# Routed experts: large and small ones by turns, with the banks of PSUM shared out anew

## The chip, the cores and the metric

The kernel runs on one core of one Trainium2 chip. Its measure is the device time of one execution in microseconds; the median of three runs before the change is 2690.89 us (2690.01 to 2691.46).

## What is computed

A stack of layers over 256 tokens of width 1024 (state space mixer, cross attention, gated MLPs, attention, recurrent hybrids), then a mixture of experts, then a last norm. The change touches only the experts:

```
logits = x @ w_router                     # 256 x 8
top_v, top_i = top_k(logits, 2)           # two experts a token
comb = sum(one_hot(top_i) * softmax(top_v))
y = sum over 8 experts of comb[:, e] * (silu(x @ wg[e]) * (x @ wu[e])) @ wd[e]
```

`wg` and `wu` are 1024 x 3584, `wd` is 3584 x 1024, all f32. The kernel computes products to f32 accuracy with the chip's rounded type fp32r: each f32 operand is split in a high part and a rest, and three of the four products are summed.

## The kernel before

**Experts and slots.** Each expert computes only its own tokens, gathered into slots. The experts are sorted by their count of tokens (except that the first to run is expert 0 in any case), and run in the order `RANKS` of that list. `CAPS` says how many slots each has in the order of running: 128, 128, 64, 128, 128, 64, 128, 64. More tokens than slots would start a second round under an `If` (it isn't entered for these inputs). With 128 slots, high part and rest of the gathered tokens are two operands (`gx`, two tiles). With 64 they stand side by side in one operand of 128 columns, so that one matmul does two products; its two halves are added later by a matmul with a doubled identity (`twice`, in `turn_small`). So an expert of 128 slots needs three matmuls for each block of weights, one of 64 slots two, while the weights to be loaded and converted are the same.

**Steps.** An expert runs in `NG` = 7 steps of 512 of its 3584 hidden columns. `up(x, g, mid)` loads two tiles of 1 MB of the gate weights and two of the up weights and accumulates `eg` and `eu` in a bank of PSUM each; `mid` is called between the two. `step_down` does the down projection of the step before that (`late`): two more tiles of 1 MB, accumulated over all seven steps in two banks `eacc`. Between them the product `ea` (or, with 64 slots, the copies `es`) is transposed by `turn` or `turn_small` into a bank `ept` and split. Every tile of 1 MB is one DMA from SP's queue into a raw buffer and is converted in two halves: ACT casts `whi` (L475), DVE subtracts `wlo` (L476), and the raw buffer is free again. There are `W_BUFS` = 4 converted halves of each kind, so the two engines are at most four halves ahead of PE. `raw_tile` deals raw buffers out by turns: 4 in `ring`, 6 in `raw2`, 3 in `raw3` during the experts.

**Start and end of an expert.** `places(es)` gathers tokens for the one or two experts of a group: it builds selections `pm`, multiplies them with the normed tokens into four banks `mpg`, which ACT and DVE read into `gx`. It is called after step 3 of the expert ahead. `places_back`, at step 4, transposes the selection for the way back into a bank `mpt`. After the last down projection, `back` scales `eacc` into `eyh` and `eyl`, scatters them with eight matmuls through four banks `esc`, and DVE adds these to the residual.

**Order.** The loop in `moe_round` runs over the eight experts one after the other, and over seven steps inside; `GROUPS` says only which experts are gathered together. The framework's planner sets each engine's order from the program's order (earlier instructions have priority), its own costs and the buffers that are free at that point, and it may start a later matmul while an earlier one lacks an operand. On the chip each engine's queue then runs in that fixed order.

**Banks.** PSUM's eight banks are two sets of four: `ps` holds `eacc`, `ept`, `mpg`, `mpt2` and `esc`; `wv` holds `eg` and `eu`.

Of the kernel before, what the change touches and what calls it, by code (L numbers as in the profile page):

```python
# [19 lines left out]
P = 128  # L20
# [8 lines left out]
NE = 8  # L29
# [2 lines left out]
RANKS = [0, 1, 5, 2, 3, 6, 4, 7]  # L32
SMALL = 64
CAPS = [P if r < 5 else SMALL for r in RANKS]
GROUPS = [[0], [1, 2], [3, 4], [5, 6], [7]]

STAGES = ["ssm", "xa0", "ffn0", "cf", "xa1", "ffn1", "ab", "cd", "hy0", "sw", "hy1", "moe", "final"]

# [193 lines left out]

RAW_BUFS = 4
W_BUFS = 4
N_T1 = (13, 6, 4)
N_T2 = (14, 4, 12)
N_SM = 20
LD = 2
FIN = 0
LEAD = 2  # L240
MORE_RAW = (6, 3)
CF_PE = [11, 12, 12, 12, 15, 15, 18, 19]
MP = 3

# [2 lines left out]
def hybrid_stack_kernel(ctx: ExitStack, tc: tile.TileContext, A, out, voff, coff, stages=STAGES):  # L247
# [66 lines left out]
    def g4(name, shape, dt=F32):  # L314
        if "attn" in pools:
            return pools["attn"].tile(list(shape), dt, tag="g4", name=name, bufs=6)
        return pools["work"].tile(list(shape), dt, tag="g4", name=name, bufs=5)

    def sm(name, shape, dt=F32):
        return pools["work"].tile(list(shape), dt, tag="sm", name=name, bufs=N_SM)  # L320
# [1 line left out]
    def ps(name, shape=(P, 2, T)):  # L322
        return psum.tile(list(shape), F32, tag="ps", name=name, bufs=4)
# [7 lines left out]
    def f32v(ap):  # L331
        return ap.bitcast(F32)
# [1584 lines left out]
    def x_by_tokens():  # L1917
        px = [ps("xtp", (P, 512)) for _ in range(4)]
        for t in range(2):
            for k in range(KD):  # L1920
                pe.transpose(px[2 * t + k // 4][:, (k % 4) * P : (k % 4 + 1) * P], xT[:, k, t * P : (t + 1) * P], ident)
        for i in range(4):
            act.copy(xtok(i // 2, i % 2), px[i])
# [4 lines left out]
    def moe_round(rnd, hth, htl, sel0, sel, comb, rest=None):  # L1928
# [30 lines left out]
        def places(es):  # L1959

            w = len(es) * P
            pm = [t1("pm", (P, T), F32R) for _ in range(2)]
            for t in range(2):
                for u, e in enumerate(es):
                    c = CAPS[e]
                    dve.tensor_scalar(
                        pm[t][:, u * P : u * P + P].rearrange("p (a b) -> p a b", b=c),
                        bc2(iota[:, :c], P // c), (sel if e else sel0)[:, t, e : e + 1], 0.0, op0=OP.is_equal, op1=OP.add,
                    )

            pgs = []
            for k2 in range(4):
                pg = ps("mpg")
                for j in range(2):
                    k = 2 * k2 + j
                    cs = slice((k % 4) * P, (k % 4 + 1) * P)
                    for t in range(2):
                        r = pm[t][:, :w]
                        mm(pg[:, j, :w], hth[2 * t + k // 4][:, cs], r, j == 0 and t == 0, False)
                        mm(pg[:, j, :w], htl[2 * t + k // 4][:, cs], r, False, j == 1 and t == 1)  # L1980
                pgs.append(pg)
            r = []
            for u, e in enumerate(es):
                c = CAPS[e]
                gx = [g4("gx", (P, KD, P), F32R) for _ in range(2 if c == P else 1)]
                for k2 in range(4):
                    ks = slice(2 * k2, 2 * k2 + 2)
                    o = u * P
                    hi = gx[0][:, ks, :c]
                    lo = gx[1][:, ks, :] if c == P else gx[0][:, ks, c:]  # L1990
                    act.copy(hi, pgs[k2][:, :, o : o + c])
                    dve.tensor_sub(lo, pgs[k2][:, :, o + P - c : o + P], f32v(hi))
                r.append((e, gx, [None, None], [p[:, u * P : u * P + P] for p in pm], c == P))
            return r

        def places_back(x):

            e, pm = x[0], x[3]
            pb = t1("pb", (P, T), F32R)
            pt = ps("mpt2")  # L2000
            for t in range(2):
                pe.transpose(pt[:, 0, t * P : (t + 1) * P], f32v(pm[t]), ident)
            for t in range(2):
                mm(pt[:, 1, :8], f32v(pm[t]), comb[:, t, :], False, t == 1)
            act.copy(pb, pt[:, 0, :])
            g = sm("gsl", (P, 1))
            dve.tensor_copy(g, pt[:, 1, e : e + 1])
            x[2][:] = [pb, g]

        def up(x, g, mid):  # L2010
            e, gx, big = x[0], x[1], x[4]
            po = [wv("eg"), wv("eu")]
            po = [a.rearrange("p a b -> p (a b)") for a in po]
            s = []
            for i, src in enumerate(("moe_g", "moe_u")):
                if i and mid:
                    mid()
                for c in range(2):
                    wt = load_e(src, e, 2 * g + c)
                    for k4 in range(4):  # L2020
                        k = 4 * c + k4
                        whi, wlo = wt[k4 // 2]
                        cs = slice((k4 % 2) * 512, (k4 % 2 + 1) * 512)
                        for a in gx:
                            mm(po[i], a[:, k, :], whi[:, cs], k == 0 and a is gx[0], False)
                        mm(po[i], gx[0][:, k, :], wlo[:, cs], False, k == KD - 1)
                if not big:
                    s.append(t2("es", (P, 512)))
                    act.copy(s[i], po[i])
            if not big:  # L2030
                return s
            a = t2("ea", (P, 512))
            act.activation(a, po[0], AF.Silu)
            dve.tensor_mul(a, a, po[1])
            return a

        def turn(a):
            pt = ps("ept", (P, 512))
            for j in range(4):
                pe.transpose(pt[:, j * P : (j + 1) * P], a[:, j * P : (j + 1) * P], ident)  # L2040
            ah, al = t2("eah", (P, 512), F32R), t2("eal", (P, 512), F32R)
            split(pt, ah, al)
            return ah, al

        def turn_small(s):

            pt = ps("ept", (P, 2, 4, SMALL))
            for i in range(2):
                for j in range(4):
                    mm(pt[:, i, j, :], s[i][:, j * P : (j + 1) * P], route["twice"], i == 0 and j == 0, i == 1 and j == 3)  # L2050
            a = pools["work"].tile([P, 4, SMALL], F32, tag="eas", name="eas", bufs=2)
            act.activation(a, pt[:, 0], AF.Silu)
            dve.tensor_mul(a, a, pt[:, 1])
            ax = t2("eax", (P, 4, P), F32R)
            split(a, ax[:, :, :SMALL], ax[:, :, SMALL:])
            return ax
# [29 lines left out]
        def back(x, acc):  # L2086
            pb, gs = x[2]
            yh = [t2("eyh", (P, 512), F32R) for _ in range(2)]
            yl = [t2("eyl", (P, 512), F32R) for _ in range(2)]
            for n in range(2):  # L2090
                act.activation(yh[n], acc[n], AF.Copy, scale=gs)
                dve.scalar_tensor_tensor(yl[n], acc[n], gs, f32v(yh[n]), op0=OP.mult, op1=OP.subtract)
            for n in range(2):
                for t in range(2):
                    po = ps("esc", (P, 512))
                    mm(po, pb[:, t * P : (t + 1) * P], yh[n], True, False)
                    mm(po, pb[:, t * P : (t + 1) * P], yl[n], False, True)
                    dve.tensor_add(xtok(t, n), xtok(t, n), po)
                    if x[0] == NE - 1:
                        act.activation(t2("fsq", (P, 512)), xtok(t, n), AF.Square, accum_out=ss[:, t, n : n + 1])  # L2100

        def step_down(late):
            x, g, a, acc = late
            if acc is None:
                acc = [ps("eacc", (P, 512)) for _ in range(2)]
            (down if x[4] else down_small)(x, g, a, acc)
            if g == NG - 1:
                back(x, acc)
                acc = None
            return acc  # L2110

        def turned():
            if late:
                late[2] = (turn if late[0][4] else turn_small)(late[2])

        todo = places(GROUPS[0])
        late = None
        for e in range(NE):
            x = todo.pop(0)
            acc = None  # L2120
            for g in range(NG):
                a = up(x, g, turned)
                if rest and e == 0 and g == 0:
                    rest()
                    x_by_tokens()
                if late is not None:
                    acc = step_down(late)
                late = [x, g, a, acc]
                if g == 3 and not todo and e < NE - 1:
                    todo += places(next(q for q in GROUPS if q[0] == e + 1))  # L2130
                if g == 4:
                    places_back(x)
        turned()
        step_down(late)

# [79 lines left out]
```

## Time and profile before

| | |
|---|---|
| median of 3 runs | 2690.89 us (2690.01 to 2691.46) |
| profiled execution, whole time | 2692.13 us |
| its span, first to last instruction | 2690.4 us |
| mean granted TensorE clock | 0.991 |
| experts, first `up` to the end of the last down projection | 1709 to 2673 us of the span |

A row that begins with an engine's name on the page gives its busy time and share of the span. The windows view gives the same for stretches of the span, with the count of instructions in brackets, then the granted clock, the busy share of the 16 DMA engines and GB/s. Matmul records overlap, so PE's busy time is more than what its work needs; the distance from one start to the next tells the pace. "PEld" is the load of weights into TensorE.

### The profile page before, as it was taken

The numbers are of one execution on the slowest core, as the hardware profiler recorded it, in microseconds if no ns is written. First come the engines' busy times: TensorE is split into PE (matmuls) and PEld (weight loads), VectorE is DVE, ScalarE is ACT, GpSimd is POOL, SyncE is SP. The second block draws the span as 40 slices with busy tenths as digits, with TensorE's granted clock in tenths as the row PEclk, the third lists the DMA queues.
The fourth block names the chain that finished last, engine by engine and source line by source line (L and its number), as shares of the span: only waits on it lengthen the run. The fifth ranks groups of instructions, "written<-read, shape, count | busy, mean of one in ns | idle before, by whom it ended". The sixth has DMA issues, their size and how long they took to land. (4 is left out here: it accounts for less than half of the span.)

```text
span 2690.4 us, 44857 instructions
## 1 busy us (share of the span) xinstructions
PE 2613.4 (97%) x17220; PEld 2340.0 (87%) x17220; DVE 2197.2 (82%) x3408; ACT 1733.0 (64%) x2605; POOL 13.6 (1%) x85
## 2 busy tenths in 40 slices
PE   8999999999989999999999999999999999999997
PEld 8999899998889989998999999888876778767875
DVE  8987587789668777677885568889999888999898
ACT  5765465655656555455654456677788777787787
POOL 0000000000000000000000000000000000000000
PEclk9999999999999999999999999999999999999999
DMA  7245345433435543342655545799999999999993
GB/s 265 99 158 182 132 168 190 160 110 125 166 105 186 188 148 130 118 157 101 266 188 189 188 167 199 268 339 357 363 373 394 352 346 341 360 406 367 343 380 151
DMA packets 87343, 620.33 MB, mean 231 GB/s; under 512 B 9937, under 2 KB 10193, under 8 KB 12881
## 3 DMA queue, kind: packets, MB, share of 16 engines
q1 hardware_dynamic: 86688, 616.83, 62.0%
q8 instruction: 137, 2.24, 0.3%
q14 instruction: 86, 0.70, 0.1%
q10 hardware_dynamic: 432, 0.56, 0.1%
HBM read 616.30 MB, written 1.05 MB: 229 GB/s over the span
## 5 line engine op out<-in xcount | busy, mean ns | idle before, releaser
L476 DVE TENSOR_TENSOR wlo<-raw,whi 128x1024 fp32r<-128x1024 f32 (+1 forms) x1164 | 1387.9, 1219 | 321.0 <-ACT whi L475 315.4
L475 ACT CAST whi<-raw 128x1024 fp32r<-128x1024 f32 (+1 forms) x1164 | 1190.2, 1049 | 559.7 <-PE wv L329 293.8
L329 PE MATMUL wv<-hh,whi 128*128 128x256 f32 x2400 | 678.8, 284 | 14.8 <-ACT hh L674 14.7
L329 PE MATMUL wv<-hh,wlo 128*128 128x256 f32 x2400 | 675.1, 283 | 3.8 <-DVE wlo L476 3.7
L329 PE MATMUL wv<-hl,whi 128*128 128x256 f32 x2400 | 678.1, 283 | 0.5 <-DVE hl L675 0.4
L329 PEld LDWEIGHTS wv<-hh,whi 128*128 128x128 f32 x2400 | 456.9, 191 | 16.7 <-ACT hh L674 15.9
L329 PEld LDWEIGHTS wv<-hh,wlo 128*128 128x128 f32 x2400 | 455.9, 191 | 5.6 <-DVE wlo L476 5.4
L329 PEld LDWEIGHTS wv<-hl,whi 128*128 128x128 f32 x2400 | 457.2, 191 | 2.4 <-DVE hl L675 1.3
L329 PE MATMUL eu<-whi,gx 128*128 128x512 f32 x728 | 245.8, 400 | 0.0
L329 PE MATMUL eg<-whi,gx 128*128 128x512 f32 x728 | 244.7, 398 | 0.0
L329 PE MATMUL eg<-wlo,gx 128*128 128x512 f32 x448 | 184.4, 412 | 10.2 <-DVE wlo L476 9.9
L329 PE MATMUL eu<-wlo,gx 128*128 128x512 f32 x448 | 184.8, 413 | 5.0 <-DVE wlo L476 4.3
L329 PEld LDWEIGHTS eg<-whi,gx 128*128 128x128 f32 x728 | 136.7, 189 | 29.5 <-ACT whi L475 0.6
L329 PE MATMUL acc<-fh,whi 128*128 128x256 f32 x576 | 161.6, 281 | 0.1
L329 PE MATMUL acc<-fl,whi 128*128 128x256 f32 x576 | 161.6, 281 | 0.0
L329 PE MATMUL acc<-fh,wlo 128*128 128x256 f32 x576 | 161.3, 280 | 0.0
L329 PEld LDWEIGHTS eu<-whi,gx 128*128 128x128 f32 x728 | 135.3, 188 | 27.0 <-ACT whi L475 0.9
L329 PEld LDWEIGHTS eg<-wlo,gx 128*128 128x128 f32 x448 | 84.3, 188 | 51.9 <-DVE wlo L476 34.5
L850 DVE SCALAR_TENSOR_TENSOR cv<-pad,vec,cv 128x256 f32<-128x256 f32 x288 | 124.9, 478 | 1.9 <-ACT cv L847 1.0
L329 PEld LDWEIGHTS eu<-wlo,gx 128*128 128x128 f32 x448 | 84.2, 188 | 40.4 <-DVE wlo L476 23.3
L329 PE MATMUL eacc<-whi,eah 128*128 128x512 f32 x280 | 110.6, 395 | 0.0
L329 PE MATMUL eacc<-whi,eal 128*128 128x512 f32 x280 | 110.5, 395 | 0.0
(568 smaller groups left out, 4220.8 us busy)
## 6 DMA issues: line engine op xcount, KB each, us to landing
raw<-moe_u SPq DMA_DIRECT2D x112, 1024.0 KB, 6.0
raw<-moe_g SPq DMA_DIRECT2D x112, 1024.0 KB, 6.1
raw<-moe_d SPq DMA_DIRECT2D x111, 1024.0 KB, 5.8
raw<-ffn_in SPq DMA_DIRECT2D x44, 1024.0 KB, 4.8
raw<-sw_in SPq DMA_DIRECT2D x28, 1024.0 KB, 4.9
raw<-ffn_out SPq DMA_DIRECT2D x22, 1024.0 KB, 4.8
raw<-hy_in SPq DMA_DIRECT2D x20, 1024.0 KB, 4.9
raw<-ssm_in SPq DMA_DIRECT2D x18, 1024.0 KB, 5.0
```

The source lines that it names most:

```text
L329: return pe.matmul(o, l, r, start=start, stop=stop, skip_group_check=True)
L475: act.copy(hi[:, cs], raw[:, cs])
L476: dve.tensor_sub(lo[:, cs], raw[:, cs], f32v(hi[:, cs]))
L850: dve.scalar_tensor_tensor(y, pad[:, j, 4 - s : 4 + T - s], taps[i], y, op0=OP.mult, op1=OP.add)
```

## The change

The main loop goes over groups, then steps, then the experts of the group, so the two experts of a pair take turns step by step. Groups are regrouped so that each pair is one expert of 128 and one of 64 slots; the first and the fourth expert run alone. Two pairs of `eacc` are kept at once, in the four banks `ps`; all else goes to the four banks `wv`. The next group is gathered after step 3 of all experts of the current one. Three tile pools grow by a buffer or more and the raw buffers shrink from 13 to 12.

```diff
-GROUPS = [[0], [1, 2], [3, 4], [5, 6], [7]]
+
+GROUPS = [[0], [1, 2], [3], [4, 5], [6, 7]]
...
-N_T1 = (13, 6, 4)
-N_T2 = (14, 4, 12)
+N_T1 = (13, 6, 5)
+N_T2 = (14, 4, 13)
...
-MORE_RAW = (6, 3)
+MORE_RAW = (6, 2)
...
-        return pools["work"].tile(list(shape), dt, tag="g4", name=name, bufs=5)
+        return pools["work"].tile(list(shape), dt, tag="g4", name=name, bufs=6)
...
-                pg = ps("mpg")
+                pg = wv("mpg")
...
-            pt = ps("mpt2")
+            pt = wv("mpt2")
...
-            pt = ps("ept", (P, 512))
+            pt = wv("ept").rearrange("p a b -> p (a b)")
...
-            pt = ps("ept", (P, 2, 4, SMALL))
+            pt = wv("ept").rearrange("p a (m s) -> p a m s", s=SMALL)
...
-                    po = ps("esc", (P, 512))
+                    po = wv("esc").rearrange("p a b -> p (a b)")
...
         def step_down(late):
-            x, g, a, acc = late
-            if acc is None:
-                acc = [ps("eacc", (P, 512)) for _ in range(2)]
-            (down if x[4] else down_small)(x, g, a, acc)
+            x, g, a = late
+            if g == 0:
+                accs[x[0]] = [ps("eacc", (P, 512)) for _ in range(2)]
+            (down if x[4] else down_small)(x, g, a, accs[x[0]])
             if g == NG - 1:
-                back(x, acc)
-                acc = None
-            return acc
+                back(x, accs.pop(x[0]))
...
+        accs, late = {}, None
         todo = places(GROUPS[0])
-        late = None
-        for e in range(NE):
-            x = todo.pop(0)
-            acc = None
+        for i, es in enumerate(GROUPS):
+            xs = todo
             for g in range(NG):
-                a = up(x, g, turned)
-                if rest and e == 0 and g == 0:
-                    rest()
-                    x_by_tokens()
-                if late is not None:
-                    acc = step_down(late)
-                late = [x, g, a, acc]
-                if g == 3 and not todo and e < NE - 1:
-                    todo += places(next(q for q in GROUPS if q[0] == e + 1))
-                if g == 4:
-                    places_back(x)
+                for x in xs:
+                    a = up(x, g, turned)
+                    if rest and x[0] == 0 and g == 0:
+                        rest()
+                        x_by_tokens()
+                    if late is not None:
+                        step_down(late)
+                    late = [x, g, a]
+                    if g == 4:
+                        places_back(x)
+                if g == 3 and i + 1 < len(GROUPS):
+                    todo = places(GROUPS[i + 1])
```

## Rows read from the trace of the kernel before

**Rows 1.** The page: busy us, share of the span and instructions by engine.
```profile
PE 2613.4 (97%) x17220; PEld 2340.0 (87%) x17220; DVE 2197.2 (82%) x3408; ACT 1733.0 (64%) x2605; POOL 13.6 (1%) x85
```

**Rows 2.** Windows, one an expert: length, busy by engine, clock, DMA share, GB/s.
```profile
core 0: us, PE busy (x) PEld busy (x) DVE busy (x) ACT busy (x) POOL busy (x), PEclk, DMA share, GB/s
1709.20:1848.40 139.20, 139.20 (x634) 113.20 (x634) 126.40 (x160) 108.24 (x121) 0.00 (x0) 0.99 0.90 341
1848.40:1968.40 120.00, 120.00 (x533) 96.74 (x532) 111.35 (x106) 95.43 (x103) 0.00 (x0) 1.00 0.95 362
1968.40:2082.60 114.20, 109.31 (x511) 81.70 (x511) 108.24 (x116) 94.66 (x121) 0.00 (x0) 1.00 0.98 384
2082.60:2207.50 124.90, 124.00 (x547) 99.07 (x546) 110.50 (x108) 91.92 (x102) 0.00 (x0) 1.00 0.95 356
2207.50:2334.20 126.70, 125.05 (x563) 99.59 (x562) 111.95 (x114) 94.22 (x110) 0.00 (x0) 1.00 0.92 346
2334.20:2446.30 112.10, 107.12 (x479) 77.55 (x478) 105.65 (x107) 93.86 (x114) 0.00 (x0) 1.00 0.98 394
2446.30:2573.10 126.80, 125.05 (x563) 99.40 (x563) 111.99 (x110) 94.26 (x106) 0.00 (x0) 1.00 0.93 347
2573.10:2673.40 100.30, 95.04 (x430) 68.38 (x430) 95.12 (x97) 84.90 (x106) 0.00 (x0) 1.00 0.71 281
```

**Rows 3.** Windows of two single steps: a large one (128 slots), a small one (64).
```profile
2179.30:2196.50 17.20, 17.20 (x77) 13.88 (x76) 15.00 (x14) 12.88 (x14) 0.00 (x0) 1.00 0.95 365
...
2404.70:2419.90 15.20, 14.65 (x65) 10.30 (x64) 14.51 (x16) 13.27 (x17) 0.00 (x0) 1.00 1.01 423
```

**Rows 4.** Order of time, PE: start, length, instruction, count, [idle before].
```profile
2265.55 0.28 PE L329 MATMUL mpg<-pm,mtl 128*128 128x256 f32 x1
2265.67 0.28 PE L329 MATMUL mpg<-pm,mth 128*128 128x256 f32 x1
...
2410.26 0.63 PE L329 MATMUL eacc<-wlo,eax 128*128 128x512 f32 x2
2410.72 0.63 PE L329 MATMUL eacc<-whi,eax 128*128 128x512 f32 x2
2411.19 0.55 PE L329 MATMUL ept<-twice,es 128*128 128x64 f32 x4
2411.55 0.72 PE L329 MATMUL eacc<-wlo,eax 128*128 128x512 f32 x2
```

**Rows 5.** Waits, 1709 to 2674 us: who for whom, us in total, times, longest.
```profile
DVE wlo L476 <- ACT whi L475: 53.2, 155, 1.7
PEld eg L329 <- DVE wlo L476: 34.5, 64, 1.1
...
PEld eu L329 <- DVE wlo L476: 23.3, 56, 1.1
```

**Rows 6.** Waits of SP's queue, then of DVE, 1700 to 2691 us.
```profile
SPq L1942 <- DVE wlo L476: 630.0, 270, 6.4
...
DVE eal L491 <- ACT eah L490: 8.6, 9, 1.9
```

**Rows 7.** Order of time in the small step of rows 3: ACT, then DVE.
```profile
2404.70 0.59 ACT L2029 COPY es<-eg 128x512 f32<-128x512 f32 x1 [1.10 <-PE eg L329]
...
2406.57 4.63 DVE L476 TENSOR_TENSOR wlo<-raw,whi 128x1024 fp32r<-128x1024 f32 x4 [0.33 <-ACT whi L475]
```

**Rows 8.** Groups of DVE instructions by shape, 1700 to 2691 us: busy, mean ns, idle before.
```profile
L2098 DVE TENSOR_TENSOR xT<-xT,esc 128x512 f32<-128x512 f32 x32 | 19.9, 679 | 0.4 <-PE esc L329 0.4
...
L1992 DVE TENSOR_TENSOR gx<-mpg,gx 128x256 fp32r<-128x256 f32 x20 | 8.0, 417 | 0.0
L1966 DVE TENSOR_SCALAR pm<-direct,selp 128x128 fp32r<-128x128 f32 x14 | 3.7, 280 | 0.0
L1992 DVE TENSOR_TENSOR gx<-mpg,gx 128x128 fp32r<-128x128 f32 x12 | 3.5, 289 | 3.1 <-ACT gx L1991 2.8
```

**Rows 9.** The page, DMA issues: count, KB each, median us to landing.
```profile
raw<-moe_u SPq DMA_DIRECT2D x112, 1024.0 KB, 6.0
```

## The prediction, made before the changed kernel was run

> **What bounds the kernel now.** I read the page first, for the engines' shares, then the windows view by expert, then by single steps, then the waits, and last the order of time inside one small step.
>
> The page says PE 97%, DVE 82% [rows 1]. That is a mean over stages with different limits, and the change touches only the experts, the last 964 us. I cut them where the first product of `back` starts (ACT's `eyh`), so each window is one expert's down projections with the up projections of its steps 1 to 6 and step 0 of the next one. The windows come in two kinds [rows 2]. Experts of 128 slots (the second, fourth, fifth and seventh row) take 120.0 to 126.8 us, DVE is busy for 110.5 to 112.0 of it. Experts of 64 slots (third, sixth, eighth) take 114.2, 112.1 and 100.3 us with 108.2, 105.7 and 95.1 us of DVE. Weights are the same for both kinds: 42 transfers of 1 MB, 84 halves that ACT casts and DVE subtracts.
>
> Single steps show which engine waits [rows 3]. A large step is 17.2 us, PE 17.20, DVE 15.00. A small one is 15.2 us, DVE 14.51, PE 14.65. PE's busy time is no measure here: matmul records of 0.63 us for a pair start 0.46 us apart [rows 4], so a matmul takes 0.23 us of PE's time, not 0.39. By that pitch a large step's 72 matmuls and 4 transposes fill its 17.2 us (72 x 0.23 = 16.6, plus 0.4): PE binds it. A small step has 48 and 8 short ones at 0.36 us per four: 11.0 + 0.7 = 11.8 us of 15.2. There DVE binds. The waits agree: PE's weight loads wait 34.5 us for `wlo` before gate matmuls and 23.3 before up matmuls, while DVE waits 53.2 us for `whi`, whose cast in turn waits for PE to leave one of the four converted halves [rows 5]. So PE idles in small experts and DVE in large ones, and neither can lend its time, for only four halves lie between them.
>
> No compute engine waits for a raw tile in that list, and SP's queue itself stands 630 us waiting for `wlo`, that is for a raw buffer to come free [rows 6]. Transfers are ahead of their use. The granted clock is 0.99 to 1.00 in all eight windows [rows 2], so it explains nothing here.
>
> **The change part by part.**
>
> *Turns within a pair.* One large and one small step now follow each other. Before they cost 17.2 + 15.2 = 32.4 us. After, DVE needs 15.0 + 14.5 = 29.5 us, PE 17.2 + 11.8 = 29.0 us. Does a ring of four halves carry the difference over? In the large step DVE makes a half in 15.0/12 = 1.25 us while PE takes 17.2/12 = 1.43: it gains 17.2/1.25 - 12 = 1.8 halves. In the small step PE takes 11.8 us, in which DVE makes 11.8/1.21 = 9.8, 2.2 short. Both fit a ring of which one half is in use. So DVE becomes the bound, at 29.5 us if it never waits. It will wait: in the small step where it is already the bound it idles 0.33 us after ACT, which stood 1.10 us for PE's gate sums [rows 7], and more such gaps make up the rest; 15.2/14.51 = 1.048. 29.5 x 1.048 = 30.9, a gain of 1.5 us a pair of steps, 21 of them: 31 us. The cast that makes DVE wait is held by the in-order ACT queue, and everything behind it (the next casts) waits too.
>
> *The whole pairs.* Steps are not all: what `back` and `places` ask of DVE lay partly under PE's time in large experts and no longer does. So I take the whole windows. Six of them are in pairs (all but the first and fourth row): 700.1 us, DVE 644.3 [rows 2]. Of the gathers, those for one large and one small expert leave the pairs: 4 x 0.417 + 4 x 0.289 us of `gx` and four of 0.28 us for `pm`, 4.0 us [rows 8]. DVE keeps 640.3. Between 1.048 and the ratio of the three small windows, 326.6/309.0 = 1.057, I take the second, because it holds the ends of experts as well: 676.8. Gain 23.3 us. Both ends: 640.3 (DVE without a gap, gain 59.8) and 700.1 (no overlap, gain 0).
>
> *The gathers that move.* The fourth expert, alone in its group, now gathers for two: 32 matmuls of 256 columns, 0.12 us each [rows 4], 3.8 us on PE, which binds there. In the first expert it was so before. Cost 3.8 us. In the pairs the same matmuls go from PE, which has time over: nothing back.
>
> *Banks.* `eacc` keeps four banks, two for each of the pair. `ept`, `mpg`, `mpt2` and `esc` come to the four that `eg` and `eu` had to themselves. In a plain step this asks for nothing new: `ept` needs the product `ea`, and that has read both old banks, so there is `eg`, `eu`, `ept` and one bank over. The gathers want four at once, and the next gate matmul then waits until `gx` is read. Below: 0, since matmuls of the gather can fill PE's waits. Above: the eight DVE reads, 8 x 0.417 = 3.3 us at each of four gathers, 13 us [rows 8]. The nearest row is the fifth window, gathering for two with two banks free: 126.7 us against 124.9 for the fourth [rows 2], where 3.8 us more of gather and 16 fewer up matmuls (3.7 us) should leave the same: 1.8 us of waits. I take that once more in the first and in the fourth expert, where PE binds: 3.6 us, and nothing in the pairs, where PE has 1 to 2 us over per pair. `back` had two free banks before, and two more after `eyl`; it has about as many now: 0, at most the 2.5 us of its four additions [rows 8] in each of eight. The Trainium skill speaks against this part ("Perfetto Trace Analysis", Optimizing Tensor Performance): groups of matmuls should rotate through banks so that the reading of one overlaps the next group, and here six uses share four. By it alone the upper ends above would hold, 13 + 20 us, and the gain of 23 would be gone; rival 3 is that case.
>
> *One raw buffer less.* 13 become 12. SP waits for buffers, not the data for SP, and a transfer lands in 6.0 us [rows 9]; 12 buffers at 2.6 us are 31 us of lead. Cost 0. At 12 tiles in 30.9 us the pairs ask for 12 x 1.049 MB = 407 GB/s for longer than any stretch so far. A small step already takes 6 in 15.2, 414 GB/s, and the sixth window held 394 over 112 us [rows 2, 3]. By that rate a pair of steps can't go below 30.4 us, just under my 30.9. The Trainium skill ("DMA: Bandwidth & Descriptors", Where 436 GB/s comes from) has the HBM side bind at some 358 GB/s per core. That would make 12.58/0.358 = 35.1 us of a pair of steps, 2.7 more than now; the trace's 394 and 414 contradict it for this core alone.
>
> *The rest.* `g4` 5 to 6, `t1` 4 to 5, `t2` 12 to 13 hold what a pair keeps alive (three `gx` with three coming); 0. The first gather no longer needs a bank that `mpx` holds, but its fourth bank waits for `mpr`: within 1 us either way, 0 taken. The last steps, from `up` of the last expert on, are nearly as before.
>
> **Sum.** 23.3 - 3.8 - 3.6 = 15.9 us. The profiled execution took 2692.13 us (span 2690.4 and 1.7 around it): 2676.2. The median of the runs is 1.24 lower, so I predict 2675 us.
>
> **Rivals.**
>
> 1. *As forecast*, DVE binds the pairs with the loss of today's small experts: 2665 to 2684 us. Chance 0.50.
> 2. *More.* With a large step between, sums for ACT are long done when it comes to them, and the gaps of [rows 7] close. Then the transfer rate is next, 30.4 us: 21 x 2.0 = 42 us, less 7.4: 2656 us, and down to 2640 if the rate goes higher. For: every wait of the small step gets 17 us of other work. Against: PE and DVE both have under 2 us over in 31, so each late release now hits one of them. 0.19.
> 3. *Slower: the shared banks.* A transposed tile holds its bank until DVE has subtracted `eal`; if the planner lets gate or up matmuls reach their turn before that, PE stands with its queue behind it, casts wait for PE, and DVE has no half to work on. It would be seen in every step: 7 x (2 + 6) = 56. DVE waited 8.6 us for `eah` in 9 of 35 steps [rows 6], 1 us each; 1 us in every step makes 56 - 16 = 40 us, 2731. It decides from 16/56 = 0.3 us a step. Against: the count of banks above. 0.13.
> 4. *No change.* PE and DVE are so evenly loaded that each waits in both kinds of step: today's waits of ACT in a small step (1.10 and more) reach DVE whole, and a pair of steps stays at 32 us: 2686 to 2696. 0.16.
> 5. *Slower: transfers bind.* If the rate that lasts is the 362 GB/s of the second window, 34.8 us a pair of steps, 21 x 2.4 = 50 us and 7: 2748. It speaks against it that small steps ran at more [rows 3], 414 GB/s. 0.02.
>
> **How the numbers follow.** Faster by over 0.2% (5.4 us, about what can be told here) holds nearly all of 1 and 2 and an eighth of 4: 0.70. Within 0.2%: most of 4 and the slow edge of 1: 0.15. Slower: 3, 5: 0.15. The range must leave out at most 0.2: 2650 to 2692 leaves the lower part of 2 (0.05) and 3 and 5 (0.15).
>
> **What would show it.** Right: windows of the three pairs near 677 us in sum, DVE busy above 93% in them, a pair of steps about 31 us, PE waiting for `wlo` spread over both kinds; the fourth expert 3 to 7 us longer. Wrong in the banks: PE idle before `eg`, `eu` or `ept` with a release by `eal`, `gx` or the addition of `back`. Wrong in the transfers: casts that wait for raw tiles and SP no longer for `wlo`. Wrong in the ring: DVE busy under 91% in the pairs while `whi` waits for PE.

## The result, and the profile after

The changed kernel is slower: 2719.73 us in the median (2716.16 to 2722.3, four runs) beside 2690.45 (2689.42 to 2691.46) for the kernel before on the same chip, a ratio of 1.0105 [1.0093, 1.0117]. I had forecast 2675 and a range of 2650 to 2692.

The page's line of busy times answers to [rows 1]. But for 18 us more of PE's overlapping records, nothing on it tells the two kernels apart.

```profile
PE 2631.4 (97%) x17220; PEld 2337.3 (86%) x17220; DVE 2194.7 (81%) x3408; ACT 1731.1 (64%) x2605; POOL 13.6 (0%) x85
```

The windows of the changed kernel, cut as [rows 2] were: the first expert, the first pair, the fourth expert alone, the second pair, the third pair (length, then busy time by engine, clock, DMA share, GB/s).

```profile
1711.70:1850.00 138.30, 138.30 (x626) 112.41 (x626) 126.09 (x160) 107.57 (x121) 0.00 (x0) 0.99 0.90 343
1850.00:2089.00 239.00, 232.22 (x1042) 176.75 (x1042) 215.51 (x216) 187.87 (x220) 0.00 (x0) 1.00 0.95 367
2089.00:2220.00 131.00, 128.87 (x580) 102.76 (x578) 114.86 (x120) 93.97 (x108) 0.00 (x0) 1.00 0.89 336
2220.00:2466.60 246.60, 237.08 (x1042) 174.89 (x1040) 217.21 (x218) 189.91 (x226) 0.00 (x0) 1.00 0.94 359
2466.60:2703.10 236.50, 223.52 (x962) 163.38 (x960) 204.46 (x202) 176.28 (x207) 0.00 (x0) 0.99 0.79 308
```

The pairs sum to 239.0 + 246.6 + 236.5 = 722.1 us. They were 700.1 and should have become 676.8. DVE works 637.2 us in them (I had 640.3), so it idles 84.9. The clock is 0.99 to 1.00. The fourth expert took 131.0 for 124.9, 6.1 more where I had 5.6.

Inside the pairs the kernel has two speeds. Two windows of a pair of steps, one small and one large, early in the first pair and late in the third:

```profile
1880.00:1911.00 31.00, 30.82 (x140) 24.02 (x139) 29.17 (x28) 26.33 (x30) 0.00 (x0) 1.00 0.98 387
2526.60:2560.50 33.90, 32.62 (x142) 23.80 (x140) 29.65 (x29) 26.21 (x31) 0.00 (x0) 1.00 0.94 375
```

The first two pairs of steps take 30.9 and 31.3 us, just my forecast of 30.9. Most later ones take 33.9, 1.5 more than one large and one small step took before (17.2 + 15.2 = 32.4, [rows 3]). Work is the same (DVE 29.2 and 29.7), so what differs is a wait. First a pair of steps at 33.9, in order of time, ACT, then DVE, then PE; in brackets the idle time before and who ended it:

```profile
2591.96 0.39 ACT L2053 ACTIVATE eas<-ept 128x256 f32<-128x256 f32 x1 [4.34 <-PE ept L330]
...
2592.38 0.42 DVE L2054 TENSOR_TENSOR eas<-eas,ept 128x256 f32<-128x256 f32 x1 [2.56 <-ACT eas L2053]
2593.31 1.23 DVE L477 TENSOR_TENSOR wlo<-raw,whi 128x1024 fp32r<-128x1024 f32 x1 [0.51 <-ACT whi L476]
...
2586.76 0.63 PE L330 MATMUL eg<-whi,gx 128*128 128x512 f32 x2
2587.22 1.67 PE L330 MATMUL ept<-twice,es 128*128 128x64 f32 x14
2588.70 0.48 PE L330 MATMUL eg<-wlo,gx 128*128 128x512 f32 x1
...
2591.60 0.33 PE L330 MATMUL ept<-twice,es 128*128 128x64 f32 x2
```

PE begins the turn of the small expert (`ept`) only after the first gate matmuls of the next, large step. It does 14 of its 16 records at once, then twelve of gate matmuls, and the last two 4.4 us later. ACT's next instruction in its fixed order reads that tile and stands for 4.34 us; the casts of `whi` behind it stand too, and DVE, which has nothing else to read, idles 2.56 us. In a fast pair of steps ACT stands a fifth of that:

```profile
1906.97 0.38 ACT L2053 ACTIVATE eas<-ept 128x256 f32<-128x256 f32 x1 [0.92 <-PE ept L330]
```

The waits of the changed kernel (1709 to 2704 us; total, times, longest) put this read at their head:

```profile
ACT eas L2053 <- PE ept L330: 66.7, 21, 4.3
...
DVE wlo L477 <- ACT whi L476: 42.1, 126, 1.5
DVE eas L2054 <- ACT eas L2053: 38.6, 18, 2.6
```

In the kernel before the same read stood far down the list:

```profile
ACT eas L2052 <- PE ept L329: 11.3, 20, 1.8
```

### The profile page after: what moved, and what is told of

It is laid out like the page before. It is cut to its first block, busy times and chain, and to the rows that moved or that the text cites. A ratio compares the mean times of both kernels' runs of the same rounds, so it can differ in the third digit from the quotient of the medians.

```text
span 2720.3 us, 44871 instructions
## 1 busy us (share of the span) xinstructions
PE 2631.4 (97%) x17220; PEld 2337.3 (86%) x17220; DVE 2194.7 (81%) x3408; ACT 1731.1 (64%) x2605; POOL 13.6 (0%) x85
## 5 line engine op out<-in xcount | busy, mean ns | idle before, releaser
L330 PEld LDWEIGHTS eu<-wlo,gx 128*128 128x128 f32 x448 | 84.1, 188 | 54.4 <-DVE wlo L477 38.5
```

Source lines behind the costliest of these rows:

```text
L330: return pe.matmul(o, l, r, start=start, stop=stop, skip_group_check=True)
```

## The experiments

Three theories stood at the start, and a fourth was formed on the way. **H**: the read of `ept` at the head of ACT's queue is the loss, and the turns by themselves give what I forecast. **L**: the ring of four halves is too small for the swing between the steps. **R**: sharing the banks costs in every step by their number as such, wherever the turn stands. **A**, formed on the way: it is the order as a whole. The shared banks change the order that the planner writes, and every read of PSUM that stands at the head of ACT's or DVE's fixed queue before its matmuls are done costs DVE time. Medians stand with the ratio to the kernel before on the same chip.

**The turn at another place in the changed kernel.**

e1: the small turn's matmuls held behind the last gate matmul (`behind` is an order of issue, no wait of its own).

```diff
-                    mid()
+                    with behind([last] if late and not late[0][4] else ()):
+                        mid()
...
-                        mm(po[i], gx[0][:, k, :], wlo[:, cs], False, k == KD - 1)
+                        last = mm(po[i], gx[0][:, k, :], wlo[:, cs], False, k == KD - 1)
```

> The changed kernel, but the eight small matmuls that turn a 64-slot expert (turn_small) are held behind the last gate matmul of the step in which they stand, as one block, instead of being split by the planner into seven early ones and a last one twelve gate matmuls later. Same work, same banks, same turns. Theory H (a held cast: ACT's silu of the turned sums stands up to 4.3 us for that last matmul, the casts behind it wait, DVE runs dry): no such wait over 1.5 us in any of the 21 pairs of steps, a pair of steps about 31 us as in the five of the changed kernel's trace where the wait was 0.9, whole 2678 to 2692 us. Theory R (the shared banks cost in every step): where eight short matmuls stand changes little, 2710 to 2722. Theory L (PE and DVE too evenly loaded for four converted halves): the same, 2710 to 2722.

2715.81 us, 1.0092 [1.0079, 1.0106]. The turn is whole again, but ACT still stands 3.7 us for it, since its own order has not changed. Pair of steps 33.8. H had 2678 to 2692 and missed.

e2: the small turn ahead of the gate matmuls.

```diff
-                if i and mid:
+                if i == (0 if late and not late[0][4] else 1) and mid:
```

> The changed kernel, but a 64-slot expert is turned before the gate matmuls of the next step in the program's order, so the eight small matmuls fall between up and down matmuls, earlier than in e1. H: the silu finds its sums ready, waits under 1 us, and ACT may place it earlier; 2672 to 2690 us, at or below e1. R and L: 2710 to 2722.

2711.76 us, 1.0079 [1.0065, 1.0093]. ACT's wait at `eas` fell to 2.1, and a new one of 1.8 came at the read of `eg`; pair of steps 33.5. H missed again.

e5: each turn in its own step, right behind `up`.

```diff
-                if i and mid:
-                    mid()
...
-                    a = up(x, g, turned)
+                    a = up(x, g, None)
+                    own = [x, g, (turn if x[4] else turn_small)(a)]
...
-                    late = [x, g, a]
+                    late = own
...
```

> The changed kernel, but each turn (both kinds) comes in the program right after its own up step, ahead of the down projection and of the next step's gate and up sums, so that it asks for its bank before they do, as the turn could in the kernel before with banks of its own. Theory A (the shared banks cost because the planner gives them out in the program's order: behind the next step's two sums the turn comes late, and ACT waits for it): the turn's matmuls lie between up and down matmuls as they did before, its silu waits under 1 us, 2665 to 2695 us. R (the number of banks as such): 2710 to 2722. L: 2700 to 2716.

2713.78 us, 1.0085 [1.0072, 1.0099]; pair of steps 33.6, with waits of ACT of 1.4 at `eas`, 2.0 at `ea`, 1.9 at `eah`, 1.5 at `es`. A had 2665 to 2695 and missed. Three places, and the time stays: in e1 the wait keeps its read, in e2 and e5 it comes up at others.

**The banks alone.** e3 has the loop and the groups of the kernel before, and only the banks of the change.

```diff
-                pg = ps("mpg")
+                pg = wv("mpg")
...
-            pt = ps("mpt2")
+            pt = wv("mpt2")
...
-            pt = ps("ept", (P, 512))
+            pt = wv("ept").rearrange("p a b -> p (a b)")
...
-            pt = ps("ept", (P, 2, 4, SMALL))
+            pt = wv("ept").rearrange("p a (m s) -> p a m s", s=SMALL)
...
-                    po = ps("esc", (P, 512))
+                    po = wv("esc").rearrange("p a b -> p (a b)")
```

> The kernel before, expert after expert with its old groups, and of the change only the banks: transposes, gathers, ways back and scatters use the four banks of the gate and up sums, the accumulators keep the other four. R: slower by 0.3 us or more in each of the 56 steps, 2705 to 2730 us. H: the plain steps never need a fifth bank; a few us at gathers and ends of experts, 2686 to 2700 us, unless the planner orders the turn anew as it did in the changed kernel.

2720.07 us, 1.0109 [1.0094, 1.0124]: the whole loss, with the experts still one after the other. So with these banks the new loop gains nothing on balance. Small steps take 16.7 to 17.1 us instead of 15.2, plain large ones still mostly 17.2 to 17.6.

e6 is e3 with each turn in its own step, as e5.

> e3 (the kernel before with the banks alone changed) with each turn right after its own up step, as in e5. A: small steps fall from 16.7-17.1 us back to about 15.2, whole 2690 to 2698 us. R: as e3, 2715 to 2722. L says nothing of it, since no turns are taken between experts.

2724.57 us, 1.0122 [1.0106, 1.0137]; ACT stands 1.2 at most `eas`, small steps 16.4. A (2690 to 2698) missed. e8 is e3 with the turn of a small expert ahead of the next gate matmuls, as e2.

> e3 (the kernel before with the banks alone changed), with the turn of a 64-slot expert ahead of the next step's gate matmuls in the program's order, so that it asks for its bank before them. PE's order around the turn is then that of the kernel before, number for number, with the banks shared. A: small steps back at 15.2 to 15.5 us, silu waits 0.2 to 0.5 us, whole 2690 to 2700. R (the number of banks as such): small steps stay at 16.4 to 17.1, whole 2712 to 2725. L says nothing of it.

2701.91 us, 1.0041 [1.0027, 1.0054]. PE's order is now that of the kernel before, ACT waits 0.2 at `eas`, small steps are back at 15.2. So 18 us of the 29 were the place of one matmul group in PE's order. The steps are as A had them, the total 1.9 us above its band; R, with 2712 to 2725, falls.

Then each use of the shared banks alone, in the kernel before. e11 moves `esc` only, e12 `ept` only, e13 `mpg` and `mpt2` only, each by its lines of the diff above.

> The kernel before with one edit: back's results come from the four banks of the gate and up matmuls. If the ends of the experts are what remains of the banks' price in e8 (11 us over eight ends): about 1.4 us at each end, total 2699 to 2706. If the gathers' banks (mpg, mpt2) are what remains, or the turn's: 2689 to 2694.

> The kernel before with one edit: the transposed tile of both turns (ept) comes from the four banks of the gate and up matmuls. If the turn's place costs the 18 us that e8 gave back: small steps at 16.7 to 17.1 us, total 2704 to 2713. If the price needs all the uses together: 2689 to 2697.

> The kernel before with one edit: the gathers' tiles (mpg, mpt2) come from the four banks of the gate and up matmuls. What is left of 29 us after 18 for the turn and 6 for the additions is 5: 2693 to 2699, all of it at the gathers. By my prediction's bounds, 3.6 (taken) to 13 us: 2694 to 2704. If the uses add up otherwise: 2689 to 2692.

e11: 2696.89 us, 1.0021 [1.0012, 1.0031]. e12: 2718.54, 1.0104 [1.0089, 1.012]. e13: 2688.89, 0.9994 [0.9985, 1.0003]. By the ratios that is 6 us, 28 and nothing: the transposed tile alone costs what the change costs. I had expected less of it (18) and something of the gathers (5); the two subtractions had left to the gathers what was the turn's. And e11 with its 6 came out below the 2699 to 2706 of its own band. By the windows e12 loses 2.5 us in the four large experts and 24 in the three small ones, which took 114.2, 112.1 and 100.3 us before [rows 2] and now:

```profile
1965.80:2086.60 120.80, 111.90 (x511) 80.36 (x510) 108.97 (x116) 94.33 (x120) 0.00 (x0) 1.00 0.95 363
...
2340.70:2462.20 121.50, 109.72 (x479) 76.18 (x478) 106.53 (x107) 93.77 (x114) 0.00 (x0) 1.00 0.97 365
...
2589.00:2697.20 108.20, 96.97 (x431) 67.52 (x430) 95.84 (x97) 84.93 (x106) 0.00 (x0) 1.00 0.68 260
```

One small step of e12: its window, then PE, ACT and DVE in order of time.

```profile
2400.80:2417.60 16.80, 14.99 (x65) 10.06 (x64) 14.66 (x16) 13.24 (x17) 0.00 (x0) 1.00 0.99 374
```

```profile
2410.62 0.40 PE L329 MATMUL eg<-whi,gx 128*128 128x512 f32 x1
2410.86 1.90 PE L329 MATMUL ept<-twice,es 128*128 128x64 f32 x16
...
2412.79 0.39 ACT L2052 ACTIVATE eas<-ept 128x256 f32<-128x256 f32 x1 [2.34 <-PE ept L329]
...
2413.20 0.42 DVE L2053 TENSOR_TENSOR eas<-eas,ept 128x256 f32<-128x256 f32 x1 [0.94 <-ACT eas L2052]
2414.14 4.63 DVE L476 TENSOR_TENSOR wlo<-raw,whi 128x1024 fp32r<-128x1024 f32 x4 [0.52 <-ACT whi L475]
```

Before, PE strewed the turn in pieces of 2 to 4 records between up and down matmuls [rows 4], and ACT read it with hardly a wait:

```profile
2412.70 0.39 ACT L2052 ACTIVATE eas<-ept 128x256 f32<-128x256 f32 x1 [0.23 <-PE ept L329]
```

In this step of e12 all 16 records stand behind the next step's first gate matmul. As the code reads, that is why: `up` asks for its two banks before `mid` asks for the turn's, and from one set of banks the planner would hand them out in the order of the program. Its own rule for that is not shown here, but e8 bears it out: the program's order changed, PE's followed, and the wait went.

The 6 us of `esc` are at the experts' ends. PE's first rows there in e11:

```profile
2208.58 0.73 PE L329 MATMUL esc<-eyh,pb 128*128 128x512 f32 x2 [0.31 <-ACT eyh L2091]
2209.37 0.74 PE L329 MATMUL esc<-eyl,pb 128*128 128x512 f32 x2
2210.11 0.73 PE L329 MATMUL esc<-eyh,pb 128*128 128x512 f32 x2
2211.44 0.73 PE L329 MATMUL esc<-eyl,pb 128*128 128x512 f32 x2 [0.60 <-DVE eyl L2092]
```

Before, the same eight matmuls lay strewn among nine gate matmuls with no idle time ahead of any:

```profile
2208.24 0.73 PE L329 MATMUL esc<-eyh,pb 128*128 128x512 f32 x2
2208.81 0.39 PE L329 MATMUL eg<-wlo,gx 128*128 128x512 f32 x1
...
2209.74 0.63 PE L329 MATMUL esc<-eyl,pb 128*128 128x512 f32 x2
```

**The readers held back.** e4 is e1 with the read of `eas` held on ACT behind the four casts of the up weights, which are loaded ahead of the turn for it.

```diff
+                small = i == 1 and late and not late[0][4]
+                wts = [load_e(src, e, 2 * g + c) for c in range(2)] if small else None
...
+                    with behind([last, cast[0]] if small else ()):
+                        mid()
...
```

> e1, and the silu of the turned sums is held on ACT behind the casts of all four halves of the up weights that follow (both their tiles are loaded before the turn in the program's order). In e1 the silu kept its old place and stood 3.7 us, so e1 did not take the wait away; this does. H: no wait of the silu over 1 us, DVE's 2.6 us of idle time before it gone, a pair of steps 31 to 32 us, whole 2665 to 2690. R, as a loss in every step that has nothing to do with this silu: 2705 to 2720. L: as one wait goes another takes its place, 2700 to 2716.

2716.94 us, 1.0098 [1.0082, 1.0113]. ACT's wait at `eas` is 0.9 in nearly all steps, the total of DVE's waits there 0.7 us instead of 38.6, and the pair of steps still takes 33.8: DVE now stands 1.9 us at the product `ea`, which waits for `eu`. H as the single wait falls.

e9 is e4 with that product held behind two subtractions of the first down tile.

```diff
+                pre[y[0], gy] = load_e("moe_d", y[0], 2 * gy)
+            with behind(subs[-1:] if late else ()):
+                dve.tensor_mul(a, a, po[1])
...
```

> e4, and DVE's product of the large expert (ea) is held behind the two conversions of the first down tile that follow, which the first pairs of steps had ahead of it and the later ones, 3 us longer, had not. Theory A, in the form that single readers of PSUM at the head of a fixed queue cost the time: DVE's wait for the last up matmul (1.9 us) goes, a pair of steps 31 to 32.3 us, whole 2672 to 2697. L: the wait turns up elsewhere, 2705 to 2718.

2700.33 us, 1.0036 [1.0022, 1.005]; a pair of steps 32.6. Both lie just above what A had (32.3, 2697). With two readers moved, two thirds of the loss are gone.

**The ring.** e7 is the changed kernel with five converted halves (and 11 raw tiles).

> The changed kernel with five converted halves of weights in place of four during the experts, and one raw buffer less for the room (11; tiles land over 20 us before their use). e1, e2, e4 and e5 took away the wait of the silu in four ways and a pair of steps stayed at 33.3 to 33.9 us. Theory L (the ring of four can't carry what DVE gains in a large step over to the small one): a pair of steps falls to 31 to 32.5 us, whole 2675 to 2705. Theory A (the order in which the planner gives banks out, and the fixed queues that follow from it): unchanged, 2710 to 2722.

2720.37 us, 1.0108 [1.0092, 1.0123]: nothing. e10 is e9 with five.

> e9 with a fifth converted half (and one raw tile less). Theory A with the ring as what is late next (the wait of 1.47 us that e9's pair step still has, a cast standing for PE's eu while the turn's records run, goes): pair step 31 to 32 us, total 2675 to 2697. Rival, the ring is no limit there either, as in e7: pair step 32.6, total 2698 to 2703. A result below 2690 would beat the kernel before as well.

2703.03 us, 1.0042 [1.0028, 1.0056]: nothing again. ACT comes earlier to its reads and stands there longer (`eas` 2.3 for 0.9, `es` 2.6 for 1.5). e14 has six halves (10 raw tiles), and the two readers held one instruction further (shown against e10).

```diff
-                    with behind([last, cast[0]] if small else ()):
+                    with behind([last, casts[-2]] if small else ()):
...
-            with behind(subs[-1:] if late else ()):
+            with behind(subs[-1 - c :][:1] if late else ()):
...
```

> e10 with six converted halves (raw tiles 10), `eas` held behind a cast of the small down tile as well, the product of `ea` behind one subtraction more. If the order on ACT and DVE together with the stock of halves holds the pair step at 32.6: 31 to 32 us, total 2670 to 2692. If PE and DVE bind it by themselves, whatever the stock: 32.4 to 32.8, total 2697 to 2706. If ten raw tiles are too few: casts wait for raw tiles, above 2706.

2693.48 us, 1.0008 [0.9999, 1.0018], no difference from the kernel before that can be told. The pair of steps came to 31.5, as expected of the order with the stock of halves; the total missed that band by 1.5 us. Pairs of steps in e9 and in e14:

```profile
2490.20:2522.80 32.60, 31.84 (x141) 24.09 (x140) 29.71 (x29) 26.50 (x30) 0.00 (x0) 1.00 0.99 398
```

```profile
2516.20:2547.70 31.50, 30.74 (x142) 24.37 (x141) 29.33 (x29) 25.89 (x30) 0.00 (x0) 1.00 1.00 402
```

e16 gives six halves to the kernel before (11 raw tiles for its 13).

> The kernel before with six converted halves instead of four (raw tiles 11 instead of 13), nothing else. If the ring limits the kernel before as well: experts of 64 slots start with a longer stock, at most 2 halves of 1.2 us at each change of kind, total 2680 to 2689. If PE binds large steps and DVE small ones whatever the ring, as the prediction has it: 2689 to 2693.

2693.97 us, 1.0009 [1.0, 1.0018]: no gain, so the ring was no limit there. How much of e14's gain is the ring and how much the readers' place was not tried apart.

**The way back's reads.** In e14 one pair of steps at each gather is much longer than the rest (39.7 us from 2310.9). ACT's row there:

```profile
2338.32 0.37 ACT L2017 CAST pb<-mpt 128x256 fp32r<-128x256 f32 x1 [5.07 <-PE mpt L333]
```

e15 writes the two reads of `mpt2` after the next `up` in the program, and holds `ea` by one subtraction more.

> e14 with the two reads of mpt2 (pb, gsl) behind the next up step, and the product of ea behind one subtraction more. If the reads at the head of ACT's and DVE's queues are the loss here too: the steps of 28.9, 26.2 and 24.1 us at the gathers lose 2 to 5 each, total 2676 to 2687, under the kernel before. If PE binds there: 2690 to 2696. If the bank of mpt2, held a step longer, stops PE: above 2696.

2692.84 us, 1.0005 [0.9996, 1.0014], and 15.9 us of waits of `pb` as in e14: the planner put the reads where they had been. A place in the program did not bind here. The other half of the edit took hold: DVE's waits at `ea` fell from 27.7 to 4.5 us, yet the plain pair of steps stayed at 31.5. So that wait did not set its length, which is a limit to A as it is put above (what PE needs, in the next section, bears on it). e17 ties the reads of `mpt2` down (shown against e15).

```diff
                     while reads:
-                        reads.pop()()
+                        with behind(casts[-6:-5]):
+                            reads.pop()()
```

> e15 with the two reads of mpt2 put behind weight casts of the next up step by an order of issue. If ACT standing for the matmuls of mpt2 (15.9 us in e14) is what is lost at the gathers: the steps of 28.9, 26.2 and 24.1 us lose 2 to 5 each, total 2676 to 2688. If PE binds there: 2690 to 2696. If the bank of mpt2 held longer stops PE: above 2696.

2685.11 us, 0.9972 [0.9963, 0.9981]: in the medians 6.4 us below the kernel before and 34.6 below the changed one. The pairs of steps at the two later gathers took 39.7 and 38.2 us in e14, 39.7 and 35.4 in e15, and here 35.0 and 32.2. Its three pairs, and one pair of steps:

```profile
1849.80:2081.10 231.30, 225.32 (x1042) 179.65 (x1042) 214.03 (x216) 184.25 (x219) 0.00 (x0) 1.00 0.96 376
...
2212.80:2446.50 233.70, 227.31 (x1040) 178.93 (x1040) 218.28 (x220) 188.32 (x226) 0.00 (x0) 1.00 0.96 379
2446.50:2667.60 221.10, 212.54 (x962) 167.62 (x960) 201.63 (x200) 173.71 (x205) 0.00 (x0) 0.99 0.85 336
2516.50:2548.00 31.50, 30.74 (x142) 24.52 (x141) 29.45 (x29) 25.90 (x30) 0.00 (x0) 1.00 1.00 397
```

The pairs sum to 686.1 us, 14.0 below the kernel before. The fourth expert still takes 6.8 us more (131.7).

## Why the prediction was wrong

**The banks are the step that failed.** I wrote of a plain step "this asks for nothing new: `ept` needs the product `ea`, and that has read both old banks, so there is `eg`, `eu`, `ept` and one bank over". The count of banks was right and beside the point. What a set of banks shared by several uses fixes is their order, and with it when PE may begin the turn. Its price was 0 in my sum; e12 measured 28 us, by the windows nearly all in the small experts, 1.1 for each of their 21 steps (the plain one shown took 1.6 more). `back`, "0, at most the 2.5 us of its four additions in each of eight", measured 0.7 an end (e11). The gathers, for which I took 3.6 us, cost nothing (e13). Of the 45 us between forecast and result the banks are 25 (e3: 29 for the 3.6 of my sum). The other 19.5 are the turns, 23.3 less the 3.8 of the gather that moves: the changed kernel is as slow as e3, which has the old loop, so that gain did not come at all.

**Rival 3 had the place and nearly the time** (2731, measured 2719.73), at a chance of 0.13. Its mechanism was another, so that the time came near is luck: it had PE standing with its queue behind a bank held until `eal`. PE does not stand there. ACT and DVE do, at the reads, while PE works on something else, and PE pays later: in the changed kernel its loads wait 38.5 us for `wlo` ahead of up matmuls and 28.2 ahead of down matmuls, where it was 23.3 and 8.8 (ahead of gate matmuls 19.0, where it was 34.5). My own list of what would show it ("PE idle before `eg`, `eu` or `ept` with a release by `eal`, `gx` or the addition of `back`") would have missed it. The Trainium skill's rule that I set against my sum ("Perfetto Trace Analysis", Optimizing Tensor Performance: rotate groups of matmuls through banks) held in its direction for the transposed tile (e12, 28 us) and the scatter (e11, 6), and not for the gathers (e13, nothing). What it names, the reading of one group under the next, was not what was lost: no engine stood for a bank in these rows.

**The turns** I priced at 1.5 us a pair of steps, 30.9 for 32.4, and 23.3 us in the pairs. The 30.9 is seen in the first two pairs of steps of the changed kernel, and 31.5 in e14 and e17; with a ring of four and two readers held it is 32.6 (e9), no gain at all, near my rival 4's 32. "Both fit a ring of which one half is in use" was an account of rates, and left out that ACT must come to each read at the right time with halves in stock. With six halves and four readers moved, 14.0 of the 23.3 us are there.

**PE's need was counted too low**, and with it "DVE becomes the bound" falls. The turn of a small expert is not "8 short ones" but 16 records. In a pair of steps of e17, where PE works almost without a break, the starts tell what each part takes:

```profile
2532.26 0.63 PE L333 MATMUL eg<-whi,gx 128*128 128x512 f32 x2
2532.73 0.39 PE L333 MATMUL eg<-wlo,gx 128*128 128x512 f32 x1
2532.96 1.89 PE L333 MATMUL ept<-twice,es 128*128 128x64 f32 x16
2534.66 0.71 PE L333 MATMUL eu<-whi,gx 128*128 128x512 f32 x2
```

Three matmuls take 0.70 us, the turn 1.70 (I had 0.7). The 120 matmuls of a pair of steps make 28.0 us, and with 0.35 for the four transposes of the large expert (from one start to the next, in the same pair) PE needs 30.1, not 29.0. That is more than DVE's 29.5 and leaves 0.8 of the forecast 30.9. So "PE has 1 to 2 us over per pair" was too much as well. At 31.5 us PE has 1.4 to spare and DVE, busy 29.45, has 2.05: PE is then the nearer bound, which fits that shorter waits of DVE changed nothing in e15.

**What held.** The fourth expert: 6.1 us for 5.6 (the 1.8 of waits that I had for the first did not come: 138.3 us for 139.2). DVE's work in the pairs: 637.2 us for 640.3. The transfers: in e17, SP's queue waits 685.8 us for `wlo` from 1709 to 2668 us, so raw tiles are still ahead. Its first two pairs moved 376 and 379 GB/s over 231 and 234 us, a pair of steps 397. The Trainium skill's 358 GB/s for a core ("DMA: Bandwidth & Descriptors", Where 436 GB/s comes from) is passed by these, as it was by the rows of before. The Trainium skill ("DMA: Bandwidth & Descriptors", Measured) gives that figure as the share when both cores of a pair stream at once; here one core ran alone, so it was no objection to my sum. The raw buffers: e17 has 10 of them, and is the fastest.

**What stays open.** Why the first pairs of steps run fast in every variant, while the program asks the same of all. In the changed kernel the turn stands whole in the first two; but e1 made it whole in every pair, and the later ones kept 33.8, so that alone is not it. e9 gives the later pairs the wait of the first ones at `eas` too (0.9) and stops at 32.6. Also the share of the ring in e14, above.

## What to carry to other kernels

Before uses of PSUM are put into one set of buffers, ask not only whether there are enough banks but which order of first use the sharing forces, and who reads each group: a read that stands at the head of an in-order engine's queue before its matmuls are done stops all that is behind it. Look for the engine that bounds the stage and follow back each of its short waits; moving one read only brings up the next, so they have to be moved together, and by an order of issue, since a place in the program may not bind. Measure each part of a change by itself when it does several things: here one use of the banks out of four cost as much as the whole. And count what an engine needs from the records of the trace, not from the calls of the program: the turn, priced as 8 matmuls, was 16.
